# Merging the two score blocks of a sliding window into one place per key

## The chip, the cores and the metric

The kernel runs on one core of a Trainium2 chip. Its time is the device time of one execution in microseconds (us), taken as the median of several runs. The engines are TensorE (PE in the profile; PEld is its weight load, which overlaps), VectorE (DVE), ScalarE (ACT), GpSimd (POOL) and SyncE (SP, which issues the DMAs). PE, DVE, ACT and POOL each work through a queue of their own in order, and they wait for one another by semaphores.

## The reference

One inference step of a two-layer hybrid decoder for a prompt of 2048 tokens and for 8 single-token samples. Each layer normalises x, multiplies by W_in (1024 x 4880), runs three mixers on slices of the result (mLSTM, Mamba-2 SSD, sliding-window attention), gates them, and multiplies by W_out (1536 x 1024) with a residual. The change is in the attention over the prompt, of which this is the core (8 query heads, 2 key/value heads of 64, window 128):

```python
def _swa_prompt(q, k, v, sinks):
    ...
    kk = jnp.concatenate([jnp.pad(k, pad)[:, :-1], k], axis=2)
    vv = jnp.concatenate([jnp.pad(v, pad)[:, :-1], v], axis=2)
    s = jnp.einsum('nbqhgd,nbkhd->nbhgqk', q, kk).astype(F32) * (Dh ** -0.5)
    ...
    mask = (delta >= 0) & (delta < WINDOW) & (kpos >= 0)
    s = jnp.where(mask[None, :, None, None], s, -jnp.inf)
    p = _sink_softmax(s, sinks.reshape(HK, G)[:, :, None, None])
    o = jnp.einsum('nbhgqk,nbkhd->nbqhgd', p.astype(vv.dtype), vv)
```

A tile of 128 queries looks at 256 keys, its own 128 and the 128 of the tile ahead of it. Query i sees its own keys 0 to i and the neighbour's keys i+1 to 127. So of each pair of keys (own c, neighbour c) a query uses one alone.

## The kernel before, in words

The prompt is worked off in blocks of 512 tokens: four blocks in each of two layers, numbered n = 0 to 7. For a block PE multiplies the normalised x by column groups of W_in (`g0`, `qk`, `v`, `o`, `z`, `x0`, `x1`, `cq`, `cz`, `bz`), in chunks of 128 rows, and the mixed result by W_out (`out`). Each product of float32 values is made of three matmuls on split values (high x high, low x high, high x low), 12 matmuls of 512 columns to a chunk (L511 and L513, in `multiply`). In the first block of each layer the weights are loaded raw and split by ACT and POOL (L488, L491); later blocks load the parts back.

Between these matmuls a planner (`pump`) puts steps of the mixers: `mix_a` (mLSTM), `mix_b` (SSD), `mix_c` (attention). Each is a generator, and a step is issued when its stream's rate allows it and when a model of the engines (`Clock`, with the costs of `COST`) says that its inputs are there. At certain chunks the remaining steps of a stream are forced out (`drain`): stream c is drained before `out` of its own block begins; for the last block, where `out` follows with nothing else to do, before the eighth chunk of `out`. So the order of every engine's queue hangs on the planner's model, and a change in a step's instructions moves rows elsewhere too.

Attention is `mix_c`. For each of a block's four tiles, `pre_c` makes rotated and normalised q and k, transposes them and splits them; the rotation of q is on POOL (L1022 to L1025). `main_c` then does the following for each half a (4 heads that share a key head). `scores`: 8 matmuls of 128x256, and one DVE instruction for each head that adds a mask, writes the 128x256 scores to memory and leaves their maximum. `exps`: one ACT exponential for each head, with the sum. `norm`: one ACT scaling for each head. `turn(a, x)`, for the two key tiles x: four transposes on PE (L1171) into one PSUM bank, then the high part by ACT (L1173) and the low part by DVE (L1174). `values(a, x)`: two matmuls of 512 columns (L1180) for each x, four in all, into one accumulator. `out`: ACT, then DVE twice (L1187 to L1189). `parts` splits the tile's values into high and low, in `vs`. The very first tile of a layer has no neighbour (`nk` is 1). The scores' key slots alternate: `sl = c % 2` is the slot of the tile's own keys. `F[2:4]` and `F[4:6]` are single buffers for the transposed parts.

Of the kernel before, what the change touches and what calls it, by code (L numbers as in the profile page):

```python
# [11 lines left out]
F32 = mybir.dt.float32  # L12
# [17 lines left out]
NEG = -1e30  # L30
# [30 lines left out]
def host_consts():  # L61
    p = np.arange(128)
    ident = np.eye(128)
    triu = (p[:, None] <= p[None, :]).astype(np.float64)
    sel = np.zeros((128, 128))
    sel[127, :] = 1.0
    prev = np.where(p[None, :] > p[:, None], 0.0, NEG)
    cur = np.where(p[None, :] <= p[:, None], 0.0, NEG)
    lim = np.where(p[:, None] <= p[None, :], -NEG, 0.0)
    own = ((p[:, None] // 6 == np.arange(12)[None, :]) | (p[:, None] >= 72)).astype(np.float64)  # L70

    border = (np.arange(1, NT + 1) * 128 // (NT + 1))[None, :]
    coarse = np.concatenate([np.where(p[:, None] >= border, NEG, 0.0), p[:, None] < border], axis=1)
    cst = np.concatenate([ident, triu, sel, prev, cur, lim, own, coarse], axis=1).astype(np.float32)
# [92 lines left out]
class Build:  # L167
    def __init__(self, tc, ctx, I, O):
# [18 lines left out]
        self.mask = cp.tile([128, 384], F32, name="mask")  # L187
# [21 lines left out]
        self.vs = cp.tile([128, 2, 2, 128], F32R, name="vs")  # L209
        self.x1 = self.dr.tile([DM, SEQ], F32, name="x1")  # L210
# [8 lines left out]
    def consts(self):  # L219
# [5 lines left out]
        nc.sync.dma_start(self.mask[:, 0:256], c[:, 384:640])  # L225
        nc.sync.dma_start(self.mask[:, 256:384], c[:, 384:512])
# [887 lines left out]
    def main_c(self, S, c):  # L1114
# [3 lines left out]
        kz, vs = self.kz, self.vs  # L1118
# [4 lines left out]
        W = 128 * nk  # L1123
        mk = self.mask[:, 128:256] if first else self.mask[:, 0:256] if sl else self.mask[:, 128:384]
        Pu = [[u[:, 0:512].rearrange("p (j c) -> p j c", c=256) for u in us] for us in (U[8:10], [S['CQ'][c], U[10]])]
# [3 lines left out]
        def P(a, j):  # L1129
            return Pu[a][j // 2][:, j % 2, 0:W]  # L1130
# [4 lines left out]
        def scores(a):  # L1135
            mxr, nm, es, den = st[a]
            for j2 in range(2):
                pS = self.mx()
                for j in (2 * j2, 2 * j2 + 1):
                    o = pS[:, (j % 2) * 256:(j % 2) * 256 + W]  # L1140
# [3 lines left out]
                for j in (2 * j2, 2 * j2 + 1):  # L1144
                    nc.vector.tensor_tensor_reduce(P(a, j), pS[:, (j % 2) * 256:(j % 2) * 256 + W], mk, 1.0, NEG,
                                                   ALU.add, ALU.max, accum_out=mxr[:, j:j + 1])
# [21 lines left out]
        def turn(a, x):  # L1168
            pT = self.mx()
            for j in range(4):  # L1170
                nc.tensor.transpose(pT[:, j * 128:j * 128 + 128], P(a, j)[:, x * 128:x * 128 + 128], self.ident)  # L1171
            PTh, PTl = self.F[2 + 2 * x:4 + 2 * x]
            nc.scalar.activation(PTh, pT, AF.Copy)  # L1173
            TT(PTl, pT, PTh.bitcast(F32), op=ALU.subtract)  # L1174

        def values(a, x):
            if x == 0:
                pO[a] = self.mx()
            for i, p in enumerate(self.F[2 + 2 * x:4 + 2 * x]):
                nc.tensor.matmul(pO[a], vs[:, x, a, :], p, start=x == 0 and i == 0, stop=x == nk - 1 and i == 1)  # L1180
# [10 lines left out]
        def parts():  # L1191
# [3 lines left out]
            TT(parts[:, 1:3], v, parts[:, 0:4:3].bitcast(F32), op=ALU.subtract)  # L1195

        ops = [(0, 0, parts)]
        for a in range(2):
            o = 2 * a
            ops += [(o, 2, scores, a), (o + 1, 2, exps, a), (o + 2, 2, norm, a), (o + 3, 2, turn, a, 0)]  # L1200
            for x in range(nk):
                ops.append((o + 4 + x, 1, values, a, x))
                if x + 1 < nk:
                    ops.append((o + 4 + x, 2, turn, a, x + 1))
# [690 lines left out]
```

## Time and profile before

| | us |
|---|---|
| median of 3 runs (lowest to highest) | 3053.2 (3044.29 to 3054.06) |
| the profiled execution's own time | 3047.01 |
| its span, first to last instruction | 3044.9 |
| PE busy | 2944.7 |
| DVE busy | 1873.7 |
| ACT busy | 1248.7 |
| POOL busy | 720.6 |

The mean clock granted to TensorE is 0.989 of its 2.4 GHz. PE is busy for 97% of the span, in all but the first of forty slices. Matmuls are pipelined and their recorded ends overlap with the next one's start; what one costs the queue is the distance from start to start, which the chain of waits shows as it walks from one to the next.

### The profile page before, as it was taken

What the parts mean: (1) busy time and instruction counts of PE and PEld (TensorE: products, weight loads), DVE (VectorE), ACT (ScalarE), POOL (GpSimd) and SP (SyncE); (2) the same over time, 40 slices, a digit from 0 to 9 for tenths busy, and PEclk for the clock granted to TensorE, in tenths of its full rate; (3) what the DMA queues carried; (4) which work ended last, traced back from release to release, by engine and by line L of the source; (5) the groups of instructions that cost most, each with busy time, mean ns of one, the idle gap of its engine ahead of it and who ended that gap; (6) DMA issues with size and microseconds to landing.
All of it is one profiled execution on the core that took longest, in us unless ns stands there. A gap on an engine that the chain in (4) does not pass through costs nothing.

```text
span 3044.9 us, 42758 instructions
## 1 busy us (share of the span) xinstructions
PE 2944.7 (97%) x14722; PEld 2414.3 (79%) x14722; DVE 1873.7 (62%) x4630; ACT 1248.7 (41%) x3080; POOL 720.6 (24%) x808
## 2 busy tenths in 40 slices
PE   6999999999999999999999999999999999999998
PEld 5787878878778788887878778788888788888877
DVE  4249656676476764467644676576755677544774
ACT  4343554325532254324454334552354224532354
POOL 3336104341030310005330561141400222000300
PEclk9999999999999999999999999999999999999999
DMA  7865547855476454564565755587444854445533
GB/s 206 278 207 200 183 143 259 269 170 163 155 227 203 151 158 154 166 197 139 175 229 171 245 191 175 184 274 244 146 153 156 271 177 149 152 156 168 176 108 125
DMA packets 263837, 567.31 MB, mean 186 GB/s; under 512 B 67020, under 2 KB 100204, under 8 KB 263572
## 3 DMA queue, kind: packets, MB, share of 16 engines
q1 hardware_dynamic: 263620, 564.58, 57.5%
q8 instruction: 116, 1.90, 0.2%
q14 instruction: 101, 0.83, 0.1%
HBM read 434.72 MB, written 132.06 MB: 186 GB/s over the span
## 4 chain that ended last, share of the span: by engine, by line
PE 72%; DVE 10%; DMA 7%; issue 4%; POOL 3%; ACT 2%; SPq 1%; POOLq 0%; DVEq 0%; ACTq 0%
PE pj L511 30%; PE pj L513 27%; DMA wr<-in_w_in 2%; PE mx L1180 2%; PE mx L1143 2%; PE mx L1171 1%; PE mx L974 1%; POOL hl L491 1%; PE mx L1221 1%; PE mx L840 1%; PE mx L847 1%; PE mx L534 1%; PE mx L533 1%; DVE quad L649 1%; PE mx L983 1%
## 5 line engine op out<-in xcount | busy, mean ns | idle before, releaser
L513 PE MATMUL pj<-hl,xTh 128*128 128x512 f32 (+1 forms) x3072 | 959.5, 386 | 18.0 <-DVE quad L554 9.7
L511 PE MATMUL pj<-xTh,hl 128*128 128x512 f32 x2240 | 725.0, 401 | 3.3 <-ACT xTh L1228 3.1
L513 PEld LDWEIGHTS pj<-hl,xTh 128*128 128x128 f32 x3072 | 568.1, 191 | 129.5 <-DVE quad L554 11.6
L513 PE MATMUL pj<-hl,xTl 128*128 128x512 f32 (+1 forms) x1536 | 586.4, 384 | 0.0
L511 PE MATMUL pj<-parts,hl 128*128 128x512 f32 x2016 | 517.4, 404 | 10.8 <-ACT parts L1228 3.7
L511 PEld LDWEIGHTS pj<-xTh,hl 128*128 128x128 f32 x2240 | 420.9, 189 | 98.2 <-ACT xTh L1228 4.1
L511 PEld LDWEIGHTS pj<-parts,hl 128*128 128x128 f32 x2016 | 368.8, 189 | 91.0 <-DVE parts L1235 4.4
L511 PE MATMUL pj<-xTl,hl 128*128 128x512 f32 x1120 | 437.6, 400 | 0.0
L491 POOL TENSOR_TENSOR hl<-wr,hl 128x512 fp32r<-128x512 f32 (+1 forms) x208 | 283.5, 1368 | 435.0 <-ACT hl L488 376.7
L513 PEld LDWEIGHTS pj<-hl,xTl 128*128 128x128 f32 x1536 | 293.2, 191 | 52.6
L511 PEld LDWEIGHTS pj<-xTl,hl 128*128 128x128 f32 x1120 | 212.1, 190 | 44.7
L1235 DVE SCALAR_TENSOR_TENSOR parts<-quad,lp_ynw,parts 128x512 fp32r<-128x512 f32 x168 | 143.2, 855 | 164.2 <-ACT quad L1232 74.0
L488 ACT ACTIVATE hl<-wr 128x512 fp32r<-128x512 f32 (+1 forms) x208 | 126.4, 614 | 232.5 <-DMA wr<-in_w_in 75.8
L1158 ACT ACTIVATE unit<-unit,c_m,c_sc 128x256 f32<-128x256 f32 (+1 forms) x192 | 111.8, 583 | 86.5 <-DVE c_m L1149 86.4
L1228 ACT ACTIVATE parts<-quad,lp_ynw 128x512 fp32r<-128x512 f32 x112 | 80.5, 720 | 155.3 <-PE pj L511 146.4
L1174 DVE TENSOR_TENSOR parts<-mx,parts 128x512 fp32r<-128x512 f32 x124 | 84.5, 686 | 96.7 <-ACT parts L1173 94.6
L1022 POOL TENSOR_TENSOR unit<-quad,rpqn 128x256 f32<-128x256 f32 x32 | 24.1, 753 | 500.5 <-PE mx L941 225.7
L649 DVE SCALAR_TENSOR_TENSOR quad<-quad,lp_cw,quad 128x512 f32<-128x512 f32 x192 | 140.1, 774 | 0.3
L1173 ACT ACTIVATE parts<-mx 128x512 fp32r<-128x512 f32 x124 | 73.0, 594 | 107.5 <-PE mx L1171 105.1
L1180 PE MATMUL mx<-parts,vs 128*128 128x512 f32 x248 | 103.9, 434 | 7.7 <-ACT parts L1173 4.6
L393 POOL TENSOR_TENSOR quad<-quad 128x512 f32<-128x512 f32 x24 | 33.9, 1414 | 287.6 <-ACT quad L391 286.9
L977 POOL TENSOR_TENSOR hst<-hst,X 128x512 f32<-128x512 f32 x32 | 34.0, 1063 | 240.3 <-PE mx L955 234.5
(404 smaller groups left out, 4565.2 us busy)
## 6 DMA issues: line engine op xcount, KB each, us to landing
hl<-kept SPq DMA_DIRECT2D x576, 512.0 KB
kept<-hl SPq DMA_DIRECT2D x192, 512.0 KB
wr<-in_w_in SPq DMA_DIRECT2D x144, 256.0 KB
hl<-kept SPq DMA_DIRECT2D x48, 272.0 KB
wr<-in_w_out SPq DMA_DIRECT2D x32, 256.0 KB
quad<-in_xT SPq DMA_DIRECT2D x32, 256.0 KB
x<-quad SPq DMA_DIRECT2D x32, 256.0 KB
quad<-x SPq DMA_DIRECT2D x16, 512.0 KB
```

Of the source, the lines that this page charges most:

```text
L488: nc.scalar.activation(h, raw, AF.Copy)
L491: nc.gpsimd.tensor_tensor(lw, raw, h.bitcast(F32), op=ALU.subtract)
L511: nc.tensor.matmul(ps[t], w[:, tt], a, start=st and first, stop=en and last)
L513: nc.tensor.matmul(ps[t][:, :N], a[:, tt], w[:, :N], start=st and first, stop=en and last)
L649: nc.vector.scalar_tensor_tensor(acc, u[:, j:j + 512], cw[:, j, c:c + 1], acc, op0=ALU.mult, op1=ALU.add)
L1143: nc.tensor.matmul(o, q, kz[:, a, s, 0:nk, :].rearrange("p n c -> p (n c)"), start=s == 0, stop=s == 1)
L1158: nc.scalar.activation(P(a, j), P(a, j), AF.Exp, bias=nm[:, j:j + 1], scale=head(sc, a, j), accum_out=den[:, j:j + 1])
L1173: nc.scalar.activation(PTh, pT, AF.Copy)
L1174: TT(PTl, pT, PTh.bitcast(F32), op=ALU.subtract)
L1180: nc.tensor.matmul(pO[a], vs[:, x, a, :], p, start=x == 0 and i == 0, stop=x == nk - 1 and i == 1)
L1228: nc.scalar.activation(yh.rearrange("p (t c) -> p t c", c=128), pt, AF.Copy, scale=L['ynw'][:, k:k + 1])
L1235: nc.vector.scalar_tensor_tensor(yl.rearrange("p (t c) -> p t c", c=128), blk, L['ynw'][:, k:k + 1], yh.bitcast(F32).rearrange("p (t c) -> ...
```

## The change

For every tile with a neighbour, the two scores of a pair of keys are merged into one place before the maximum. ACT copies the own block's scores of two heads out of PSUM, and DVE writes the neighbour's over them wherever the key comes later than the query (`copy_predicated` with `later`). One `tensor_reduce` then takes the four maxima of a half. From there P is 128x128 for each head and not 128x256: exponentials and scalings are half as wide, and there is one `turn` for each half and not two. The values are made right by linearity. With one merged P, the two first matmuls go against the neighbour's values for all keys; then P is masked to the own keys (`own`, two POOL multiplications by `triu`) and two more matmuls go against the difference of own and neighbour's values, `vd`, which `parts` computes and splits (one ACT and three DVE instructions more). The tiles without a neighbour add the mask and multiply once.

```diff
         def scores(a):
...
-                for j in (2 * j2, 2 * j2 + 1):
-                    nc.vector.tensor_tensor_reduce(P(a, j), pS[:, (j % 2) * 256:(j % 2) * 256 + W], mk, 1.0, NEG,
-                                                   ALU.add, ALU.max, accum_out=mxr[:, j:j + 1])
+                pS = pS.rearrange("p (j n c) -> p j n c", n=2, c=128)
+                P2 = Pu[a][:, 2 * j2:2 * j2 + 2]
+                if first:
+                    TT(P2, pS[:, :, 0], self.cur.unsqueeze(1).to_broadcast([128, 2, 128]), op=ALU.add)
+                else:
+                    nc.scalar.activation(P2, pS[:, :, sl], AF.Copy)
+                    nc.vector.copy_predicated(P2, self.later.bitcast(I32).unsqueeze(1).to_broadcast([128, 2, 128]),
+                                              pS[:, :, 1 - sl])
+            nc.vector.tensor_reduce(mxr, Pu[a], AX.X, ALU.max)
...
-        def turn(a, x):
+        def turn(a):
             pT = self.mx()
             for j in range(4):
-                nc.tensor.transpose(pT[:, j * 128:j * 128 + 128], P(a, j)[:, x * 128:x * 128 + 128], self.ident)
-            PTh, PTl = self.F[2 + 2 * x:4 + 2 * x]
+                nc.tensor.transpose(pT[:, j * 128:j * 128 + 128], P(a, j), self.ident)
+            PTh, PTl = self.F[2:4]
...
+        def own(a):
+            for p, o in zip(self.F[2:4], self.F[4:6]):
+                p, o = [x.bitcast(F32).rearrange("p (j c) -> p j c", c=128) for x in (p, o)]
+                nc.gpsimd.tensor_tensor(o.bitcast(F32R), p, self.triu.unsqueeze(1).to_broadcast([128, 4, 128]), op=ALU.mult)
+
         def values(a, x):
             if x == 0:
                 pO[a] = self.mx()
+            v = vd[:, a] if x else vs[:, sl if first else 1 - sl, a]
             for i, p in enumerate(self.F[2 + 2 * x:4 + 2 * x]):
-                nc.tensor.matmul(pO[a], vs[:, x, a, :], p, start=x == 0 and i == 0, stop=x == nk - 1 and i == 1)
+                nc.tensor.matmul(pO[a], v, p, start=x == 0 and i == 0, stop=x == nk - 1 and i == 1)
...
         def parts():
...
+            if not first:
+                old = vs[:, 1 - sl].rearrange("p a (s d) -> p (a s) d", d=64).bitcast(F32)
+                d = U[10][:, 0:128].rearrange("p (a d) -> p a d", d=64)
+                TT(d, v, old[:, 0:4:3], op=ALU.subtract)
+                TT(d, d, old[:, 1:3], op=ALU.subtract)
+                parts = vd.rearrange("p a (s d) -> p (a s) d", d=64)
+                nc.scalar.activation(parts[:, 0:4:3], d, AF.Copy)
+                TT(parts[:, 1:3], d, parts[:, 0:4:3].bitcast(F32), op=ALU.subtract)
...
-            ops += [(o, 2, scores, a), (o + 1, 2, exps, a), (o + 2, 2, norm, a), (o + 3, 2, turn, a, 0)]
+            ops += [(o, 2, scores, a), (o + 1, 2, exps, a), (o + 2, 2, norm, a), (o + 3, 2, turn, a)]
             for x in range(nk):
                 ops.append((o + 4 + x, 1, values, a, x))
-                if x + 1 < nk:
-                    ops.append((o + 4 + x, 2, turn, a, x + 1))
+            if nk > 1:
+                ops.append((o + 3, 3, own, a))
```

What this does to PE's queue, at three places. The first is a tile in the second block of layer 0. L1171 is a transpose and L1180 a values matmul of before; in the change they are L1177 and L1194, and `vd` marks the two against the difference. Before:

```order
L1180 MATMUL mx_7176<-parts_94,vs 128x512
L1171 MATMUL mx_7179<-ident,unit_90 128x128 x2
L1180 MATMUL mx_7176<-parts_95,vs 128x512
L1171 MATMUL mx_7179<-ident,unit_91 128x128 x2
L721 MATMUL mx_7217<-MB_7078,sel 128x64
L1171 MATMUL mx_7245<-ident,quad_104 128x128 x2
L1171 MATMUL mx_7245<-ident,unit_92 128x128 x2
L513 MATMUL pj_7143<-hl_7252,xTh_114 128x512
```

With the change:

```order
L1194 MATMUL mx_7353<-parts_95,vs 128x512
L1177 MATMUL mx_7372<-ident,unit_92 128x128 x3
L1194 MATMUL mx_7353<-parts_96,vs 128x512
L1177 MATMUL mx_7372<-ident,unit_92 128x128
L1194 MATMUL mx_7353<-parts_97,vd 128x512
L1099 MATMUL mx_7395<-ident,unit_90 128x128 x2
L1102 MATMUL mx_7398<-ident,quad_105 128x128 x3
L1194 MATMUL mx_7353<-parts_98,vd 128x512
```

Two sets of four transposes stood between the first half's values, the neighbour's second set and the other half's first; now one stands there. The transposes that feed these values come earlier, and 22 matmuls of 512 columns (L514, before L513) stand between them and the first row shown.

The second place is PE's queue where block n = 6 is drained, just before its `out`. Before, from the last matmul ahead of the drained steps:

```order
L513 MATMUL pj_24053<-hl_24133,xTh_114 128x512
L1180 MATMUL mx_24204<-parts_94,vs 128x512
L1171 MATMUL mx_24207<-ident,unit_90 128x128 x2
L1171 MATMUL mx_24207<-ident,unit_91 128x128 x2
L1171 MATMUL mx_24245<-ident,quad_102 128x128 x2
L1171 MATMUL mx_24245<-ident,unit_92 128x128 x2
L1180 MATMUL mx_24204<-parts_95,vs 128x512
L1180 MATMUL mx_24204<-parts_96,vs 128x512
L1180 MATMUL mx_24254<-parts_94,vs 128x512
L1180 MATMUL mx_24204<-parts_97,vs 128x512
```

With the change:

```order
L1177 MATMUL mx_24118<-ident,unit_91 128x128 x4
L1194 MATMUL mx_24132<-parts_95,vs 128x512
L1177 MATMUL mx_24146<-ident,unit_92 128x128
L1194 MATMUL mx_24132<-parts_96,vs 128x512
L1177 MATMUL mx_24146<-ident,unit_92 128x128
L1194 MATMUL mx_24132<-parts_97,vd 128x512
L1177 MATMUL mx_24146<-ident,unit_92 128x128 x2
L1194 MATMUL mx_24132<-parts_98,vd 128x512
L1194 MATMUL mx_24155<-parts_95,vs 128x512
L1243 MATMUL mx_24163<-ident,quad_102 128x128 x4
L1194 MATMUL mx_24155<-parts_96,vs 128x512
L1243 MATMUL mx_24194<-ident,quad_102 128x128 x4
```

Before, the first set of transposes was spread over the matmuls ahead of the drain; now both halves' sets stand in it, with their values right behind them. The second half's scores end 12 matmuls of 512 columns ahead of the first row shown. L1243 turns another mixer's output for `out`.

The third place is the end of the last tile of the program, with what was the last of its values. Before:

```order
L1180 MATMUL mx_27078<-parts_94,vs 128x512
L1180 MATMUL mx_27038<-parts_97,vs 128x512
L1171 MATMUL mx_27081<-ident,quad_98 128x128 x2
L1180 MATMUL mx_27078<-parts_95,vs 128x512
L1171 MATMUL mx_27081<-ident,unit_92 128x128 x2
L511 MATMUL pj_26985<-xTl_116,hl_26941 128x512
L511 MATMUL pj_26986<-xTl_116,hl_26941 128x512
L511 MATMUL pj_26987<-xTl_116,hl_26941 128x512
L1180 MATMUL mx_27078<-parts_96,vs 128x512
L1180 MATMUL mx_27078<-parts_97,vs 128x512
```

With the change:

```order
L512 MATMUL pj_26809<-xTl_117,hl_26783 128x512
L1177 MATMUL mx_26926<-ident,unit_91 128x128 x4
L1194 MATMUL mx_26940<-parts_95,vs 128x512
L1177 MATMUL mx_26954<-ident,unit_92 128x128 x4
L1194 MATMUL mx_26940<-parts_96,vs 128x512
L1194 MATMUL mx_26940<-parts_97,vd 128x512
L1194 MATMUL mx_26963<-parts_95,vs 128x512
L1194 MATMUL mx_26940<-parts_98,vd 128x512
L1194 MATMUL mx_26963<-parts_96,vs 128x512
L1194 MATMUL mx_26963<-parts_97,vd 128x512
L1194 MATMUL mx_26963<-parts_98,vd 128x512
```

Before, only the second half's second key tile was left at the end, behind three other matmuls. Now both halves' transposes and all eight values matmuls stand together, with no other matmul among them; what follows in both cases is the part of `out` that needs this tile. The change has 240 transposes fewer on PE (of 496 on L1171), 120 instructions more on POOL, and as many values matmuls as before.

## Rows read from the trace of the kernel before

**Rows 1.** The page: span; busy time, share and instructions of each engine.

```profile
span 3044.9 us, 42758 instructions
...
PE 2944.7 (97%) x14722; PEld 2414.3 (79%) x14722; DVE 1873.7 (62%) x4630; ACT 1248.7 (41%) x3080; POOL 720.6 (24%) x808
```

**Rows 2.** PE's waits: who waited for whom, us in all, times, longest.

```profile
PE mx L443 <- DVE quad L1824: 16.5, 1, 16.5
PE mx L974 <- DVE unit L969: 12.3, 6, 4.6
```

**Rows 3.** Groups of PE by line: names, shapes, count, busy, mean ns, idle before.

```profile
L1171 PE MATMUL mx<-ident,unit 128*128 128x128 f32 x372 | 70.9, 277 | 6.0 <-ACT unit L1166 5.4 <-DVE unit L966 0.6
...
L1171 PE MATMUL mx<-ident,quad 128*128 128x128 f32 x124 | 24.8, 274 | 0.0
```

**Rows 4.** The chain that ended last: start, us, what, how many.

```profile
2966.59 5.58 PE pj L511 x24
2972.17 0.23 PE mx L1180
2972.40 0.44 PE mx L1171 x4
```

**Rows 5.** Groups of DVE by line and shape: count, busy, mean ns, idle before.

```profile
L1174 DVE TENSOR_TENSOR parts<-mx,parts 128x512 fp32r<-128x512 f32 x124 | 84.5, 686 | 96.7 <-ACT parts L1173 94.6 <-PE mx L1180 1.5
L1145 DVE CUSTOM_DVE_ANT_0 unit<-mx,mask 128x256 f32<-128x256 f32 x180 | 67.8, 420 | 24.7 <-PE mx L1143 24.3
...
L1038 DVE TENSOR_REDUCE qn<-unit 128x8 f32<-128x512 f32 x32 | 21.3, 679 | 48.7 <-ACT unit L1034 48.6
...
L1145 DVE DVE_READ_ACCUMULATOR2_ANT c_m<- 128x1 f32 x256 | 21.1, 82 | 0.0
```

**Rows 6.** ACT by line: ns min/median/max, start, forms.

```profile
L1158 ACT ACTIVATE unit<-unit,c_m,c_sc x192: 477/587/605, 325.9 to 2998.2; 128x256 f32<-128x256 f32 x180, 128x128 f32<-128x128 f32 x12
...
L1166 ACT ACTIVATE unit<-unit,c_m x192: 385/494/516, 329.0 to 3000.7; 128x256 f32<-128x256 f32 x180, 128x128 f32<-128x128 f32 x12
```

**Rows 7.** ACT, groups by line and shape, as in rows 5.

```profile
L1173 ACT ACTIVATE parts<-mx 128x512 fp32r<-128x512 f32 x124 | 73.0, 594 | 107.5 <-PE mx L1171 105.1 <-DVE mst L727 1.2
...
L1104 ACT ACTIVATE kz<-mx 128x256 fp32r<-128x256 f32 x32 | 12.1, 379 | 23.2 <-PE mx L1098 23.0
```

**Rows 8.** POOL, groups by line and shape, as in rows 5.

```profile
L491 POOL TENSOR_TENSOR hl<-wr,hl 128x512 fp32r<-128x512 f32 x192 | 270.6, 1414 | 394.6 <-ACT hl L488 336.4 <-DMA hl<-kept 27.2 <-DMA wr<-in_w_in 12.0
L1024 POOL TENSOR_TENSOR quad<-quad,rpqn 128x512 f32<-128x512 f32 x32 | 42.9, 1342 | 4.4 <-ACT unit L1034 3.5
...
L979 POOL TENSOR_TENSOR unit<-unit,X 128x512 f32<-128x512 f32 x32 | 34.1, 1064 | 156.5 <-PE mx L974 151.4 <-ACT parts L1109 5.1
...
L1022 POOL TENSOR_TENSOR unit<-quad,rpqn 128x256 f32<-128x256 f32 x32 | 24.1, 753 | 500.5 <-PE mx L941 225.7 <-DVE qn L1038 208.1 <-DVE ltB L781 66.7
```

**Rows 9.** DVE line L1149: ns min/median/max.

```profile
L1149 DVE TENSOR_TENSOR c_m<-c_m,lp_nsink x64: 125/161/1199, 325.7 to 2995.4; 128x4 f32<-128x4 f32 x64
```

**Rows 10.** Instructions in order of time, POOL and DVE near 1829 us.

```profile
1828.96 1.28 POOL L491 TENSOR_TENSOR hl<-wr,hl 128x512 fp32r<-128x512 f32 x1
...
1829.06 1.20 DVE L1149 TENSOR_TENSOR c_m<-c_m,lp_nsink 128x4 f32<-128x4 f32 x1
```

**Rows 11.** PE in order of time, at the drain of block 6.

```profile
2661.42 0.50 PE L1180 MATMUL mx<-parts,vs 128*128 128x512 f32 x1 [0.71 <-ACT parts L1173]
```

**Rows 12.** PE's waits from 2880 to 2955 us, as in rows 2.

```profile
PE mx L1180 <- ACT parts L1173: 1.6, 2, 0.9
```

**Rows 13.** Stretches: length, busy PE, PEld, DVE, ACT, POOL; granted clock; DMA.

```profile
2931.00:2937.00 6.00, 5.36 (x24) 5.20 (x24) 3.13 (x15) 3.55 (x12) 0.00 (x0) 0.50 0.00 0
3008.00:3015.00 7.00, 3.89 (x17) 2.45 (x16) 3.80 (x6) 3.00 (x5) 0.00 (x0) 1.00 0.38 135
```

**Rows 14.** The chain that ended last, behind the last tile's values.

```profile
3011.71 0.60 ACT unit L1187
...
3014.55 12.97 PE pj L511 x48
```

More of the change, by code (lines that the diff above doesn't have):

```diff
@@ L66, in host_consts @@
     sel[127, :] = 1.0
-    prev = np.where(p[None, :] > p[:, None], 0.0, NEG)
+    later = (p[None, :] > p[:, None]).astype(np.float64)
     cur = np.where(p[None, :] <= p[:, None], 0.0, NEG)
@@ L73, in host_consts @@
     coarse = np.concatenate([np.where(p[:, None] >= border, NEG, 0.0), p[:, None] < border], axis=1)
-    cst = np.concatenate([ident, triu, sel, prev, cur, lim, own, coarse], axis=1).astype(np.float32)
+    cst = np.concatenate([ident, triu, sel, later, cur, lim, own, coarse], axis=1).astype(np.float32)
     inv = (10000.0 ** (-np.arange(32) / 32.0)).astype(np.float32)
@@ L186, in __init__ @@
         self.sel = cp.tile([128, 128], F32, name="sel")
-        self.mask = cp.tile([128, 384], F32, name="mask")
+        self.later, self.cur = [cp.tile([128, 128], F32, name=n) for n in ("later", "cur")]
         self.identb = cp.tile([128, 128], BF16, name="identb")
@@ L209, in __init__ @@
         self.vs = cp.tile([128, 2, 2, 128], F32R, name="vs")
+        self.vd = cp.tile([128, 2, 128], F32R, name="vd")
         self.x1 = self.dr.tile([DM, SEQ], F32, name="x1")
@@ L224, in consts @@
         nc.sync.dma_start(self.sel, c[:, 256:384])
-        nc.sync.dma_start(self.mask[:, 0:256], c[:, 384:640])
-        nc.sync.dma_start(self.mask[:, 256:384], c[:, 384:512])
+        nc.sync.dma_start(self.later, c[:, 384:512])
+        nc.sync.dma_start(self.cur, c[:, 512:640])
         t = self.U[7]
@@ L1117, in main_c @@
         QT = self.F[0:2]
-        kz, vs = self.kz, self.vs
+        kz, vs, vd = self.kz, self.vs, self.vd
         first = b == 0 and c == 0
@@ L1122, in main_c @@
         nk = 1 if first else 2
-        W = 128 * nk
-        mk = self.mask[:, 128:256] if first else self.mask[:, 0:256] if sl else self.mask[:, 128:384]
-        Pu = [[u[:, 0:512].rearrange("p (j c) -> p j c", c=256) for u in us] for us in (U[8:10], [S['CQ'][c], U[10]])]
+        Pu = [u[:, 0:512].rearrange("p (j c) -> p j c", c=128) for u in U[8:10]]
         st = [[self.s([128, 4], f"c_m{i}") for i in range(4)] for _ in range(2)]
@@ L1129, in P @@
         def P(a, j):
-            return Pu[a][j // 2][:, j % 2, 0:W]
+            return Pu[a][:, j]
         def head(x, a, j):
@@ L1139, in scores @@
                 for j in (2 * j2, 2 * j2 + 1):
-                    o = pS[:, (j % 2) * 256:(j % 2) * 256 + W]
+                    o = pS[:, (j % 2) * 256:(j % 2) * 256 + 128 * nk]
                     q = QT[a][:, j * 128:j * 128 + 128]
```

## The prediction

> **What bounds the kernel now.** I read the page first: PE is busy for 2944.7 of 3044.9 us, and no other engine passes 62% [rows 1]. Then PE's waits: of the 100 us in which it is idle, 16.5 lie at the start, before the first transposes can run, and the next longest entry is 12.3 [rows 2]. Nothing waits for long, so time is won by giving PE fewer columns to stream, and lost where PE's queue stands still. Then the groups by line, for what the edited instructions take [rows 3, 5 to 8]; the chain, for what a matmul costs PE's queue from start to start [rows 4]; and the places where the attention runs with little beside it: the drain of block 6, the start of the last block, and the last tile [rows 11 to 14].
>
> **PE: what goes.** 30 of the 32 tiles have a neighbour; each has two halves with two sets of four transposes, and the other two tiles have one set for each half: 124 sets, 496 transposes [rows 3]. With the change it is 64. A set of four costs the queue 0.44 us, as one 512-column values matmul costs 0.23 and 24 main matmuls 5.58 (0.2325 each) [rows 4]. So 60 x 0.44 = 26.4 us of queue leave PE. The upper end is the busy time of the groups, (70.9 + 24.8) / 124 = 0.77 us a set, 46 us for 60 [rows 3]; but recorded ends of pipelined matmuls overlap, so I take 0.44. Score and values matmuls stay as many and as wide. The lower end is nothing, if waits fill all that is freed.
>
> **DVE.** 240 maximum instructions of 128x256 go (0.420 each, and 0.082 for the accumulator read), and 60 subtractions of `turn` (0.686): 120.5 + 41.2 = 161.7 us [rows 5]. 120 predicated copies come. The trace has none of them; the nearest row is the maximum itself, which also streams 256 PSUM scores and a mask: 0.420. The lower end is nothing beyond the 0.082 of a one-column read, the upper twice 0.420 if the copy first has to read what it overwrites [rows 5]. At 0.420 they take 50.4. 64 reductions of 128x512 at 0.679 take 43.5 [rows 5], and 90 small operations of `parts` at most 0.42 each, 37.8. DVE ends about 30 us lighter, 20 heavier at the upper end: of 62% it is a percent either way.
>
> **ACT.** Exponentials and scalings halve in width. 240 of each go from 0.587 to 0.477 and from 0.494 to 0.385 (the minima of these rows are the 128x128 form): 26.4 + 26.2 us [rows 6]. 60 copies of `turn` go at 0.594, 35.6; 120 copies out of PSUM come at 0.379, 45.5, and 30 small ones at no more, 11.4 [rows 7]. ACT ends 31 us lighter. All this lies beside PE's main matmuls, as the sums of before do; I count nothing for it. Where the cover is gone, in a drain, the change costs or saves a single instruction's length, and there it is counted below.
>
> **POOL.** 120 multiplications of 128x512 come. By the nearest row, which also broadcasts one input, each takes 1.342 us; the ends are 1.064 and 1.414 [rows 8]. That is 161 us (128 to 170) on an engine busy for 721 [rows 1].
>
> **What hides POOL's work.** The one new wait: the last two values matmuls of a half wait for POOL, and behind them in PE's queue stand main matmuls that would be ready. From the last transpose it takes 0.594 (ACT) + 1.342 = 1.9 us to the first masked part and 3.3 to the second [rows 7, 8]. In the second block's tile the queue holds 22 + 2 matmuls and one set of transposes between the last transpose and the first of these two values: 24 x 0.2325 + 0.44 = 6.0 us [rows 4]. Cover is 4.1 us of other POOL work, three operations of 1.34. At most tiles the wait costs nothing. The cover is gone in the drains.
>
> **Drain of block 6.** Both halves now stand there together. The second half's scores end 12 matmuls, a set and a value ahead of its transposes: 2.79 + 0.44 + 0.23 = 3.5 us. What must happen in between: two copies 0.76, the last predicated copy 0.42, the reduction 0.68, three small DVE operations of 0.16 [rows 9], four exponentials 1.91, two small operations 0.32, four scalings 1.54: 6.1 [rows 5 to 7]. PE waits 2.6 us here; the wait for ACT's 0.594 lies inside it. Then the single buffer is refilled: POOL's first operation, from 0.59 to 1.94 us behind the first set, is over by then, and the second half's high part costs another 0.5 us or so. So 3.1, where before PE waited 0.7 [rows 11]: +2.4 us.
>
> **Last tile.** Four POOL operations stand in one line behind the first transposes: 0.594 + 4 x 1.342 = 6.0 us to the last values matmul. PE has a set of transposes and seven values in that time, 0.44 + 7 x 0.23 = 2.05, and stands for 3.9. The chain behind it stays: from the end of the last values at 3011.7 to the next matmul at 3014.55 are 2.9 us [rows 14]. Before, PE stood for 7.00 - 3.89 = 3.1 us around it, that is 0.2 beside this chain [rows 13]. So +3.7 us.
>
> **Start of the last block.** Values waited 1.6 us for ACT's copies [rows 12]. Half of these copies are gone, and transposes of `out` now fill in: a first wait of 0.6 is left, -1.0 us.
>
> **Sum.** -26.4 + 2.4 + 3.7 - 1.0 = -21.3, against the profiled execution's 3047.0: 3025.7 us. That execution lies 6.2 us below the median of the runs shown, 3053.2, and 2.7 above the lowest; I put the forecast between the two bases, at 3028 us.
>
> **The port between DVE and POOL.** At 1829.06 us a DVE multiplication of four columns, whose median is 0.161 us, took 1.20 while POOL was in one that began at 1828.96 and ran 1.28 [rows 9, 10]. Both its inputs are in SBUF. So a POOL operation can hold DVE for its whole length. "SBUF — State Buffer" in the Trainium skill, section "Who interferes with whom", says that a DVE instruction with two SBUF inputs contends with a GpSimd instruction that reads SBUF, and that whoever comes first has the ports for the whole instruction. By that rule, which the row agrees with, the 120 multiplications speak against the change.
>
> **Rivals.**
> 1. *POOL holds DVE.* 120 x 1.342 = 161 us more in which DVE's instructions with two SBUF inputs stand; if half of it holds one, DVE gets 80 us and gives back its 30, 1924 of 3025, 64%. DVE is not the bound, but PE waits for it, 12.3 us on L974 alone [rows 2]. POOL's busy time grows by 161/721, 22%. If all idle time of PE behind its start, 100.2 - 16.5 = 83.7 us, hung on DVE and grew by as much, it would be 18 us; at half of that 9: 3037. For it: the row above. Against it: `copy_predicated` and the subtraction of `turn` read PSUM.
> 2. *The planner's new order makes new waits.* The rows of all engines move. What a bad place costs shows at 2931 to 2937 us: PE, which had stood there before, was granted 0.50 of its clock, the lower of its two levels, 1.2 GHz, and streamed at half speed, 3 us lost in 6 [rows 13]. Together with waits like that of L974 (4.6 at longest, [rows 2]) such a place is worth about 8 us. Two of them more than before bring 3028 + 16 = 3044, no change against 3053 once the base is 3047. Against it: the freed room on PE is the same everywhere, and old places can vanish as well, up to the 12.3 us of L974, 3016.
> 3. *Values wait for POOL everywhere: slower.* POOL's queue has the rotation of the next tile's q, two operations of 0.753 and two of 1.342, 4.2 us [rows 8]. If it stands between a half's transposes and its masking, it passes the cover of 4.1 us; with the six table operations before it, or a second loaded queue in the blocks that split weights (1.414 each), the wait grows by 1.3 us for every operation over three. It decides from one such operation at 60 halves: 60 x 1.34 = 80 us would give 3108; at the 24 halves ahead of a next tile's rotation, 24 x 1.34 = 32 us and 3060, slower. Against it: in POOL's queue as ordered, what stands directly ahead of a masking is a single multiplication of another mixer, a split of weights, a memset or the other half's masking, not a rotation.
> 4. *The freed time comes back as idle:* the other mixers' DVE and ACT work or the loading of weights sets the pace, and what PE no longer streams it waits: all 26.4 us of it give 3052 and, with the two gains and losses of the drains, no change. For it: the stretches where DVE is what PE waits for. Against it: the longest such wait after the start is 4.6 us [rows 2], and DVE and ACT lose work too.
>
> **Chances and range.** The forecast (3015 to 3038) has 0.62, rival 1 0.12, rival 2 0.13 (half of it ends as no change), rival 3 0.08, rival 4 0.05. The range from 3012 to 3047 holds the sum with both bases, the good end of rival 2 and its bad end; above it lie rivals 3 and 4. A difference under 0.3%, 9 us, is what the runs of this kernel can't tell from none. Faster: 0.62 + 0.12 + half of rival 2 = 0.80, less 0.03 for the scatter of the base: 0.77. No change: half of rival 2, rival 4 and half of this scatter, 0.13. Slower: rival 3 and the other half, 0.10.
>
> **What would show it.** In the profile after, the transposes' line should have 256 instructions, PE's busy time be lower by about 26 us or more, and POOL's higher by 128 to 170. The two `vd` matmuls of a middle tile should start with no wait for POOL; at the drain of block 6 and at the last tile they should wait, about 3 and 4 us. DVE's busy time would be about 30 us lower; if it is not lower, the predicated copy or the port was mispriced. The forecast is wrong if PE's idle time grows by more than 15 us, or if a `vd` matmul waits for POOL in most tiles.

## The result, and the profile after

The kernel after takes 3016.8 us (median of 4 runs, 3012.6 to 3019.8) against 3048.7 for the kernel before beside it (4 runs, 3042.7 to 3054.1): a ratio of 0.9890, 95% interval 0.9867 to 0.9913, or 32 us less. The two profiled spans differ by 34.1 us, 3044.9 [rows 1] and 3010.8. The page of the kernel after, its part 1 (busy time, share, instructions):

```profile
span 3010.8 us, 42267 instructions
...
PE 2915.7 (97%) x14482; PEld 2386.1 (79%) x14482; DVE 1900.8 (63%) x4340; ACT 1219.5 (41%) x3170; POOL 882.7 (29%) x928
```

Against [rows 1], PE is busy 29.0 us less with 240 matmuls fewer, and its idle time falls from 100.2 to 95.1. ACT loses 29.2 us, POOL gains 162.1, and DVE, which was to lose 30, gains 27.1.

The groups of the kernel after by line, engine and shape (busy time, mean ns, idle time ahead and what ended it). Lines have shifted: the transposes of L1171 are now L1177, the values of L1180 are L1194, and L1186 is POOL's masking.

```profile
L1186 POOL TENSOR_TENSOR parts<-parts,triu 128x512 fp32r<-128x512 f32 x120 | 159.3, 1343 | 426.7 <-ACT parts L1179 405.6 <-DVE parts L1180 13.7 <-DVE rq_t L327 2.0
...
L1203 DVE TENSOR_TENSOR quad<-quad,unit 64x512 f32<-64x512 f32 x64 | 56.7, 886 | 1.7
L970 DVE SCALAR_TENSOR_TENSOR unit<-unit,unit 128x512 f32<-128x512 f32 x64 | 56.2, 919 | 0.7
L1150 DVE COPY_PREDICATED unit<-later,mx 128x256 f32<-128x256 int32 x120 | 51.1, 444 | 19.5 <-ACT unit L1149 18.5
...
L1152 DVE TENSOR_REDUCE c_m<-unit 128x4 f32<-128x512 f32 x64 | 43.7, 682 | 0.9
...
L1164 ACT ACTIVATE unit<-unit,c_m,c_sc 128x128 f32<-128x128 f32 x256 | 124.2, 487 | 78.0 <-DVE c_m L1155 77.5
...
L1172 ACT ACTIVATE unit<-unit,c_m 128x128 f32<-128x128 f32 x256 | 81.9, 394 | 17.1 <-DVE c_m L1170 16.6 <-ACT parts L1179 0.3
...
L1194 PE MATMUL mx<-parts,vd 128*128 128x512 f32 x120 | 50.8, 439 | 0.9 <-POOL parts L1186 0.7
...
L1177 PE MATMUL mx<-ident,unit 128*128 128x128 f32 x256 | 46.9, 280 | 5.5 <-ACT unit L1172 5.5
```

The 256 transposes answer to the two groups of [rows 3]. The predicated copy takes 0.444 us, the reduction 0.682, a half exponential 0.487 and a half scaling 0.394 (0.420, 0.679, 0.477 and 0.385 were assumed). The values matmuls that read `vd` waited for POOL for less than a microsecond in all 120. What became longer are instructions that the change doesn't touch, such as L1203 and L970. In the kernel before the same two groups, then L1189 and L969, read:

```profile
L969 DVE SCALAR_TENSOR_TENSOR unit<-unit,unit 128x512 f32<-128x512 f32 x64 | 51.0, 837 | 0.8
...
L1189 DVE TENSOR_TENSOR quad<-quad,unit 64x512 f32<-64x512 f32 x64 | 45.8, 716 | 1.4
```

PE's longest waits after, as in [rows 2] (us in all, times, longest):

```profile
PE mx L444 <- DVE quad L1846: 15.9, 1, 15.9
PE mx L975 <- DVE unit L970: 12.4, 6, 5.5
PE pj L514 <- DVE quad L555: 6.1, 6, 2.5
...
PE mx L1177 <- ACT unit L1172: 5.5, 1, 5.5
PE mx L1194 <- ACT parts L1179: 4.7, 3, 2.6
```

The list has the same shape as before: the start, the wait of L975 for DVE, and some entries of 4 to 6 us. No new line tops it.

The last tile in the order of time (start, duration, engine, line, idle time ahead and its releaser). It answers to [rows 13, 14]:

```profile
2971.37 0.50 PE L1194 MATMUL mx<-parts,vs 128*128 128x512 f32 x1 [1.33 <-ACT parts L1179]
2971.40 4.98 POOL L1186 TENSOR_TENSOR parts<-parts,triu 128x512 fp32r<-128x512 f32 x4 [18.25 <-ACT parts L1179]
...
2976.44 0.49 PE L1194 MATMUL mx<-parts,vd 128*128 128x512 f32 x1 [0.72 <-POOL parts L1186]
...
2979.82 2.50 PE L512 MATMUL pj<-xTh,hl 128*128 128x512 f32 x5 [2.89 <-ACT xTh L1250]
```

POOL's four operations stand in one line from 2971.40 for 4.98 us, and the last values matmul starts when the fourth is over. PE stands 1.33 us for ACT's copy, 0.22 for DVE, 0.72 for POOL, and then 2.89 for the chain behind the tile: 5.2, where it stood 3.1 before. Its values matmuls are recorded with 0.49 to 0.50 us each. That is no lower clock: the granted clock was 1.00 here, as it was around the last tile before [rows 13], where a matmul with nothing ready behind it is recorded with as much. Start to start in a full queue one costs 0.23 [rows 4]. After (columns as in [rows 13]), and then before:

```profile
2971.00:2977.00 6.00, 4.29 (x12) 1.93 (x12) 3.13 (x4) 1.55 (x4) 4.98 (x4) 1.00 0.15 62
```

```profile
3011.17 0.50 PE L1180 MATMUL mx<-parts,vs 128*128 128x512 f32 x1 [0.23 <-DVE parts L1174]
```

So the busy time of a row of lone matmuls overstates what they are worth, and idle time alone understates what such a place costs.

### The profile page after: what moved, and what is told of

Read it like the earlier page. It is cut to its first block, busy times and chain, and to the rows that moved or that the text cites. A ratio compares the mean times of both kernels' runs of the same rounds, so it can differ in the third digit from the quotient of the medians.

```text
span 3010.8 us, 42267 instructions
## 1 busy us (share of the span) xinstructions
PE 2915.7 (97%) x14482; PEld 2386.1 (79%) x14482; DVE 1900.8 (63%) x4340; ACT 1219.5 (41%) x3170; POOL 882.7 (29%) x928
## 4 chain that ended last, share of the span: by engine, by line
PE 74%; DVE 11%; DMA 7%; POOL 2%; issue 2%; ACT 2%; SPq 1%; POOLq 0%; DVEq 0%; ACTq 0%
PE pj L512 30%; PE pj L514 28%; PE mx L1194 2%; DMA wr<-in_w_in 2%; PE mx L1143 2%; PE mx L975 1%; POOL hl L492 1%; PE mx L535 1%; PE mx L534 1%; DMA kept<-hl 1%; PE mx L1243 1%; PE mx L1177 1%; DMA unit<-bcd 1%; PE mx L841 1%; PE mx L862 1%
## 5 line engine op out<-in xcount | busy, mean ns | idle before, releaser
L514 PE MATMUL pj<-hl,xTh 128*128 128x512 f32 (+1 forms) x3072 | 946.2, 383 | 11.1 <-DVE quad L555 6.1
L514 PEld LDWEIGHTS pj<-hl,xTh 128*128 128x128 f32 x3072 | 566.3, 190 | 122.2 <-DVE quad L555 7.7
L514 PE MATMUL pj<-hl,xTl 128*128 128x512 f32 (+1 forms) x1536 | 582.2, 382 | 0.0
L514 PEld LDWEIGHTS pj<-hl,xTl 128*128 128x128 f32 x1536 | 291.4, 190 | 52.3
L1186 POOL TENSOR_TENSOR parts<-parts,triu 128x512 fp32r<-128x512 f32 x120 | 159.3, 1343 | 426.7 <-ACT parts L1179 405.6
L1164 ACT ACTIVATE unit<-unit,c_m,c_sc 128x128 f32<-128x128 f32 x256 | 124.2, 487 | 78.0 <-DVE c_m L1155 77.5
L1180 DVE TENSOR_TENSOR parts<-mx,parts 128x512 fp32r<-128x512 f32 x64 | 43.9, 686 | 76.7 <-ACT parts L1179 74.5
L534 PE MATMUL mx<-hl,samS 128*66 128x512 f32 (+1 forms) x208 | 84.9, 409 | 4.5 <-ACT hl L489 4.5
L1172 ACT ACTIVATE unit<-unit,c_m 128x128 f32<-128x128 f32 x256 | 81.9, 394 | 17.1 <-DVE c_m L1170 16.6
```

Source lines behind the costliest of these rows:

```text
L514: nc.tensor.matmul(ps[t][:, :N], a[:, tt], w[:, :N], start=st and first, stop=en and last)
L534: nc.tensor.matmul(pd[:66, :N], self.samS[:, k, :], hi[:, :N], start=st, stop=False)
L1164: nc.scalar.activation(P(a, j), P(a, j), AF.Exp, bias=nm[:, j:j + 1], scale=head(sc, a, j), accum_out=den[:, j:j + 1])
L1172: nc.scalar.activation(P(a, j), P(a, j), AF.Copy, scale=den[:, j:j + 1])
L1186: nc.gpsimd.tensor_tensor(o.bitcast(F32R), p, self.triu.unsqueeze(1).to_broadcast([128, 4, 128]), op=ALU.mult)
```

## The experiments

All runs are timed against the kernel before on their own chip (medians 3049.5 to 3050.5 there). Differences below are to the kernel after: ratio minus 0.9890, times 3050.

The order of the queues is made in two places. The planner writes the steps, and then the framework's own scheduler, which has a model of durations, sorts the rows of each engine once more. To change an instruction and nothing else, both must be held: instructions that are added are hidden from the planner, and ordering edges between neighbours of one engine (they add no wait) hold all five queues as in the kernel after:

```
+        if at in self.unseen:
+            continue
...
+            for i in [mine[at]] + new.get((e, at), []):
...
+                if prev is not None:
+                    tc.add_manual_dep(i, prev.name, info(), reason="queue")
+                prev = i
```

In the three runs that are called free below, the second part is missing. Their expectations speak of held queues, but only the planner was held: 471 rows of PE's queue moved in the first and 645 in the last. The same edits were then run held.

**The transposes given back**, free, and then held:

```
             for j in range(4):
                 nc.tensor.transpose(pT[:, j * 128:j * 128 + 128], P(a, j), self.ident)
+            if nk > 1:
+                for j in range(4):
+                    nc.tensor.transpose(pT[:, j * 128:j * 128 + 128], P(a, j), self.ident)
```

> The changed kernel with every engine's queue held in its own order, and the set of four transposes written twice (60 more sets, unseen by the planner): the transposes of the kernel before, in the order of the kernel after. Theory: the gain is PE's columns, 0.44 us for a set, and what goes beyond is the new order: +26 us on 3017, 3043, ratio to before 0.998. Rival A (a set costs the queue more than its columns, the whole 32 us of the gain are these 60 sets, 0.53 each): +32, 3049, ratio 1.000. Rival B (the gain is order alone, and transposes fill time in which PE waits anyway): below +8, ratio 0.992 or less.

> As the first try, now with every engine's queue really held in the changed kernel's order (in the first calls the framework's own scheduler had still moved 471 rows of PE's queue): 60 sets of four transposes more, nothing else. Theory: PE's columns, 0.44 us a set, +26 on the kernel after; with the ratio of the kernel after, 0.989, that is 0.9975. The first try gave +20, with the order free; then order is worth 6 us here. Rival A (a set costs 0.53): 1.000. Rival B (the transposes fill waits): 0.992 or less.

Free: 3036.8 us, 0.9963 (0.9950 to 0.9976), +22 us by the ratio. Held: 3039.2, 0.9964 (0.9951 to 0.9977), +23; the intervals of the two ratios together leave 15 to 31. The page of the held run (this execution is 7 us longer than their median):

```profile
span 3044.7 us, 42750 instructions
...
PE 2946.2 (97%) x14722; PEld 2415.4 (79%) x14722; DVE 1901.8 (62%) x4340; ACT 1216.6 (40%) x3170; POOL 882.8 (29%) x928
```

The other three engines are within 3 us of the kernel after, so this is PE alone. From start to start in PE's queue, its 496 transposes fill 55.2 us in the trace and the 256 of the kernel after 28.8: 26.4 us for 60 sets, 0.44 each. (In the trace of the kernel before, in its own order, the 496 fill 50.7, 21.9 more than after.) So rival B falls (the transposes don't fill waits), and the theory's 26 lies inside the interval; rival A's 32 lies just outside it. Neither run gives back the whole gain.

**POOL's work taken away, and moved to DVE.** The first masks 2 of each 128 columns and leaves out the other 126.

```
-                nc.gpsimd.tensor_tensor(o.bitcast(F32R), p, self.triu...to_broadcast([128, 4, 128]), op=ALU.mult)
+                nc.gpsimd.tensor_tensor(o[:, :, 0:2].bitcast(F32R), p[:, :, 0:2], self.triu[:, 0:2]..., op=ALU.mult)
```

> The changed kernel, queues held, POOL's 120 multiplications cut to 2 of each 128 columns, so that the masked parts are wrong and their time on POOL is gone (a memset of the buffers at the start of each layer is added). Theory: DVE falls by the 57 us of POOL's hold to about 1844, and PE gains only the waits of the drains, 1 to 4 us: ratio 0.988. Rival (POOL holds DVE and PE waits for that): 0.986 or less.

Measured: 3014.9, 0.9887 (0.9868 to 0.9907), 1 us below the kernel after. Its page, and two of DVE's groups:

```profile
PE 2914.2 (97%) x14482; PEld 2384.6 (79%) x14482; DVE 1857.9 (62%) x4342; ACT 1215.1 (40%) x3170; POOL 753.3 (25%) x928
```

```profile
L1343 DVE TENSOR_TENSOR quad<-quad,unit 64x512 f32<-64x512 f32 x64 | 48.3, 755 | 1.7
...
L1108 DVE SCALAR_TENSOR_TENSOR unit<-unit,unit 128x512 f32<-128x512 f32 x64 | 50.7, 832 | 0.7
```

DVE falls by 42.9 us, and the two groups (L1203 and L970 of the kernel after) go back from 886 to 755 ns and from 919 to 832. So POOL did hold DVE. PE's gain from its letting go is 1 us by the ratio, and the two intervals leave 9 either way; PE is idle for 98.0 us in this trace, against 95.1 in the kernel after, so its waits in sum didn't shrink. The theory holds, and the rival by which PE waits for this finds no support.

```
-                nc.gpsimd.tensor_tensor(o.bitcast(F32R), p, self.triu...to_broadcast([128, 4, 128]), op=ALU.mult)
+                nc.vector.tensor_tensor(o.bitcast(F32R), p, self.triu...to_broadcast([128, 4, 128]), op=ALU.mult)
```

> The changed kernel, queues held, with the two multiplications of a half on DVE, directly behind its subtraction, and not on POOL. They read two inputs in SBUF, as the subtraction for xTl does (0.736 us): 120 x 0.736 = 88 us more for DVE, 57 less if POOL's hold on it goes, so DVE at about 1932, POOL at 723. Theory: no change beside other work, 2 to 4 us gained in the drains, 3013 to 3016, ratio 0.988. Rival (DVE is what PE waits for): 1.5 us more in DVE's queue for each half delays what stands behind it, +8 us or more, ratio 0.992 or above.

> The changed kernel, queues held, the two multiplications of a half on DVE directly behind its subtraction. With the order free: 3 us slower than the kernel after, DVE at 1934. Theory: what DVE takes on (88 us) and what POOL no longer holds (57) are both beside PE's work; the drains gain 2 to 3: ratio 0.988, as in the kernel with POOL's time taken away. Rival (1.5 us more in DVE's queue for each half makes PE wait): 0.991 or above.

Free: 3020.1, 0.9904 (0.9891 to 0.9917). Held: 3020.2, 0.9904 (0.9886 to 0.9922), +4 us, which these intervals can't tell from none. Page and group of the held run:

```profile
PE 2917.3 (97%) x14482; PEld 2386.1 (79%) x14482; DVE 1930.7 (64%) x4460; ACT 1214.9 (40%) x3170; POOL 727.7 (24%) x808
```

```profile
L1325 DVE TENSOR_TENSOR parts<-parts,triu 128x512 fp32r<-128x512 f32 x120 | 82.1, 725 | 0.0
```

1930.7 - 82.1 = 1848.6 us is what DVE has to do when POOL doesn't mask: 52 us under the kernel after (43 with the narrow masks, which still take some of POOL's time), and 25 under the kernel before, close to the 30 that the prediction had. The gain of 2 to 3 us in the drains that the theory wanted didn't come, nor the rival's loss with any certainty.

**POOL's work doubled**, each multiplication issued twice:

```
                 nc.gpsimd.tensor_tensor(o.bitcast(F32R), p, self.triu...to_broadcast([128, 4, 128]), op=ALU.mult)
+                nc.gpsimd.tensor_tensor(o.bitcast(F32R), p, self.triu...to_broadcast([128, 4, 128]), op=ALU.mult)
```

> The changed kernel, queues held, with each of POOL's multiplications issued twice: POOL at 1043 us. A half's second part is then over 0.594 + 4 x 1.342 = 6.0 us behind the transposes, as much as the cover of 6.0. Theory: the cover is used up, values wait a few tenths in many tiles and 1.3 to 5.4 us more in the two drains: +8 to +16 us, 3025 to 3033, ratio 0.992 to 0.995; DVE's busy time grows by another 57 us. Rival (POOL's work has free room, and PE never waits for it beside the drains): +3 to +7. Rival (POOL holds DVE and PE waits for that): over +16.

> The changed kernel, queues held, each of POOL's multiplications issued twice. With the order free this was 26 us slower than the kernel after, with DVE 48 us busier and 645 rows of PE's queue moved. Theory now: the cover is used up and DVE is held longer; of the 26 the larger part is new order, so held +8 to +14, ratio 0.992 to 0.9935. Rival (it is POOL's time itself, through late values or through DVE): +20 or more, ratio 0.9955 or above.

Free: 3043.1, 0.9978 (0.9968 to 0.9988), +27. Held: 3064.4, 1.0042 (1.0024 to 1.0060), +46. My theory falls, and the rival with 20 us or more holds. The theory missed both in its 8 to 14 us and in its claim that the new order was the larger part of the loss: with the order held the loss is larger, and the scheduler, left free, had hidden 20 us of it. The held run's page and PE's waits:

```profile
span 3061.9 us, 42382 instructions
...
PE 2933.3 (96%) x14482; PEld 2392.7 (78%) x14482; DVE 1944.5 (64%) x4340; ACT 1215.4 (40%) x3170; POOL 1047.1 (34%) x1048
```

```profile
PE mx L1335 <- POOL parts L1326: 19.5, 13, 3.0
...
PE mx L1113 <- DVE unit L1108: 13.9, 7, 5.6
```

The span grows by 51.1 us: 33.5 of idle time and 17.6 of busy time. The new entry is the first row, 13 waits of `vd` values for POOL, 19.5 us. The longest entry for DVE (L1113 is L975 of the kernel after) hardly moves, though DVE is busy for another 44 us. But summed over the list, PE's waits for DVE grow from 57.0 us (31 waits) to 67.4 (42), spread over entries that gain 2.6 at most. So the late values are the larger part of the new idle time; whether the 10 us of waits for DVE come from POOL's hold on it or only follow from the other delays was not separated. The busy time grows with the same matmuls, because PE runs longer at its lower level. Mean granted clock of the kernel after and of this one:

```profile
core 0: 3010.8 us, clock 0.987
```

```profile
core 0: 3061.9 us, clock 0.982
```

As an estimate from these rows, 0.013 of 3010.8 is 39 us lost to the clock, 0.018 of 3061.9 is 55: 16 us more, nearly the 17.6. Which stretches were lower, and after which waits, was not followed one by one.

**Other orders, same instructions.** One constant of the planner's model is changed, in the kernel before and in the kernel after:

```
-    HOP = 250.0
+    HOP = 240.0
```

> The kernel before with one constant of the planner's model, the 250 ns between two engines, set to 240: the same instructions in another order (506 rows of PE's queue moved, against 1293 by the change itself). Theory: the order alone is worth several us either way, 3 to 15 from 3049, so that the 8 to 11 us by which the gain exceeds the transposes (22 held) lie within it. Rival (the order is worth under 3 us, and the rest of the gain is ACT's and DVE's shorter work): 3046 to 3053, ratio 0.999 to 1.001.

> The kernel before with that constant at 260 (208 rows of PE's queue moved). Theory: 3 to 10 us either way from 3049. Rival: 3046 to 3053.

> The kernel after with that constant at 240 (890 rows of PE's queue moved). Theory: 3 to 15 us either way from 3017, more likely above it than below, since this order of the kernel after is 8 to 11 better than its transposes explain: 3014 to 3032, ratio 0.988 to 0.994. Rival (order is worth under 3 us): 0.988 to 0.990.

> The kernel after with that constant at 260 (259 rows of PE's queue moved). Theory: 3 to 10 us either way, 3010 to 3027, ratio 0.987 to 0.9925. Rival: 0.988 to 0.990.

Before: 1.0040 (1.0027 to 1.0053) and 1.0018 (1.0010 to 1.0027), 12 and 5 us slower than with 250. After: 3039.8, 0.9967 (0.9955 to 0.9979), and 3029.9, 0.9936 (0.9923 to 0.9948), 23 and 14 us slower. The page of the kernel after with 240 (its profiled execution is the longest of six, 8 us above their median, and that of the kernel after is 4 below its own):

```profile
span 3045.8 us, 42276 instructions
...
PE 2929.7 (96%) x14482; PEld 2392.4 (79%) x14482; DVE 1905.2 (63%) x4340; ACT 1216.4 (40%) x3170; POOL 882.5 (29%) x928
```

Of the 35 us between the two spans, 21.0 are PE's idle time (116.1 for 95.1), spread over many entries of which none gains more than 3.5, and 14.0 are busy time with the same matmuls. The rival falls, in the kernel before with 260 only just. The theory holds for the kernel before; for the kernel after its direction does, but both sizes were missed: 3 to 15 and 3 to 10 us were expected. An order is worth 5 to 23 us here, where the change is worth 32. Over the three orders the means are 3056 for the kernel before and 3029 for the kernel after, 27 us apart.

**A mended drain.** At the last tile of blocks 6 and 7 the low part's mask goes to DVE, all queues held:

```
+                e = nc.vector if S['n'] > 5 and c == 3 and k == 1 else nc.gpsimd
+                e.tensor_tensor(o.bitcast(F32R), p, self.triu...to_broadcast([128, 4, 128]), op=ALU.mult)
```

> The kernel after, queues held in its order, with one thing moved: at the last tile of blocks 6 and 7, where the steps stand in a drain, the low part's multiplication is on DVE (0.68 us in the run with all of them there) and only the high part's on POOL. In the last tile four POOL operations in one line (4.98 us) become two beside DVE's two; the last values matmul should start some 1.1 us sooner after the first transposes, and block 6 gain up to 1. Theory: 3013 to 3017, ratio 0.987 to 0.989, that is 1 to 2 us below the kernel after and hardly to be told from it; it also times the order of the kernel after once more. Rival (the drain's wait is set by ACT's copies and DVE's own subtraction): no gain, 0.989, and the last values matmul starts as late as before.

Measured: 3015.9, 0.9887 (0.9867 to 0.9907), which can't be told from the kernel after. In its last tile:

```profile
2973.84 0.51 PE L1337 MATMUL mx<-parts,vs 128*128 128x512 f32 x1 [1.32 <-ACT parts L1317]
...
2977.75 0.19 PEld L1337 LDWEIGHTS mx<-parts,vd 128*128 128x128 f32 x1 [0.36 <-DVE parts L1326]
```

From the first values matmul to the weights of the last it takes 3.9 us, against 5.1 for the same step above: 1.15 us sooner, as reckoned. At block 6 the wait for ACT's copy stayed at 2.6 us, as the rival had it. This kernel beats the kernel before and equals the kernel after. As a second timing of the same order it also bears out the 0.989.

## Why the prediction was right, and where it was wrong

**PE, what goes: right.** 60 sets at 0.44 us were put at 26.4. Start to start in the traces they fill 26.4 in the held run. By time they gave back 23, within 15 to 31.

**What hides POOL's work: right, and narrow.** The cover was put at 6.0 us for a need of 1.9 and 3.3. One masking for each part costs 1 us in all, give or take 9 (POOL's work taken away); two for each part cost 46, with 13 waits. Rival 3 was a real mechanism, kept away by the room that was left. One sign that the prediction gave didn't show: the `vd` matmuls were to wait for POOL about 3 and 4 us in the two drains, and they waited 0.7 in the last tile and not at all at block 6.

**DVE: wrong.** It was to be 30 us lighter and is 27 heavier. The new operations cost what was assumed, so the step that failed is the sum that left POOL's hold out: 43 to 52 us of it, by the runs with narrow masks and with the masks on DVE. The prediction had the mechanism as rival 1, at 80 us if half of POOL's time held one. A row in the kernel after, DVE and POOL at one place, shows how it looks:

```profile
2183.41 0.67 DVE L1202 TENSOR_TENSOR unit<-unit,mx 64x512 f32<-64x512 f32 x1
...
2185.55 0.67 DVE L1203 TENSOR_TENSOR quad<-quad,unit 64x512 f32<-64x512 f32 x1
2186.14 1.26 DVE L698 COPY li<-kvg 128x16 f32<-128x16 f32 x1
```

```profile
2183.59 1.30 POOL L1186 TENSOR_TENSOR parts<-parts,triu 128x512 fp32r<-128x512 f32 x1 [4.81 <-ACT parts L1179]
2185.70 1.68 POOL L1186 TENSOR_TENSOR parts<-parts,triu 128x512 fp32r<-128x512 f32 x1 [0.81 <-DVE parts L1180]
```

At 2186.14 a copy of 16 columns takes 1.26 us and ends as POOL's multiplication does, at 2187.38; its line has a median of 0.174. At 2183.41 an addition that reads PSUM, L1202, takes its usual 0.67 beside another. So POOL's hold isn't kept to DVE instructions with two inputs, of which the prediction spoke. "SBUF — State Buffer" in the Trainium skill, section "Who interferes with whom", says so too: a copy can run in a mode that takes both of DVE's ports, and then contends. The row agrees with it; whether this copy ran in that mode no view shows. Rival 1's price for PE, 9 to 18 us, doesn't show: with the hold gone the kernel gained 1 us, give or take 9, and PE's idle time didn't fall.

**ACT: right**, 29 us lighter for 31. **POOL: right**, 1.343 us each for 1.342, 162 in all for 161.

**The drains: mis-sized, and at block 6 by another path.** By idle time they look cheap: PE stands 5.2 us around the last tile, 2.1 more than before, and 2.6 at the drain of block 6, 1.9 more. But lone matmuls hide part of the loss in busy time, and so does a lower clock. Timed from start to start, from the first transposes of the drained steps (before: from the last main matmuls ahead) to the next main matmul behind them, the two places read as follows, block 6 first. Columns as in [rows 13]. Before:

```profile
2660.31:2666.34 6.03, 5.11 (x29) 3.46 (x27) 4.53 (x9) 5.13 (x12) 0.00 (x0) 1.00 0.35 121
3009.51:3014.55 5.04, 1.93 (x8) 0.84 (x6) 3.35 (x6) 2.16 (x5) 0.00 (x0) 1.00 0.31 104
```

After:

```profile
2622.99:2632.85 9.86, 7.21 (x24) 4.73 (x23) 6.02 (x12) 7.49 (x23) 5.21 (x4) 0.66 0.17 55
2968.93:2979.82 10.89, 5.41 (x18) 2.40 (x17) 4.54 (x7) 4.96 (x13) 4.98 (x4) 0.90 0.17 64
```

At 0.11 us for a transpose and 0.23 for any other matmul, what starts in them would take 4.0 and 1.2 us before, and 3.4 and 2.7 after. So 2.0 and 3.9 us were lost before, and 6.5 and 8.2 after: +4.5 at block 6 and +4.3 at the last tile, where +2.4 and +3.7 were forecast.

At block 6 the wait of 2.6 us came out as worked out, but by luck. The prediction had the second half's transposes wait for its scalings. In the trace the first half's values wait for ACT's copy of their transposes, which stands in ACT's queue behind the second half's four exponentials; the scalings come after it:

```profile
2622.99 0.60 PE L1177 MATMUL mx<-ident,unit 128*128 128x128 f32 x4
...
2623.56 0.49 ACT L1164 ACTIVATE unit<-unit,c_m,c_sc 128x128 f32<-128x128 f32 x1
...
2625.57 0.59 ACT L1179 ACTIVATE parts<-mx 128x512 fp32r<-128x512 f32 x1
...
2626.22 0.79 PE L1194 MATMUL mx<-parts,vs 128*128 128x512 f32 x1 [2.63 <-ACT parts L1179]
...
2626.53 1.29 ACT L1172 ACTIVATE unit<-unit,c_m 128x128 f32<-128x128 f32 x4
```

POOL doesn't stand in the list of waits there. Behind this wait PE went on at the lower level of its clock: the mean granted clock of the stretch is 0.66, where it was 1.00 before. The prediction's sum has nothing for that.

**Start of the last block: wrong sign.** A wait of 5.5 us for the scaling stands there now (L1177 in the waits above), where 1.0 was to be gained. One stands there in all three orders of the kernel after (5.5, 4.3 and 4.5 us) and in none of the three of the kernel before, which waits there in L974 (3.9, 3.9 and 5.6), so it is not a matter of one order.

**The size, 3016.8 for 3028.** The sum gave -21.3, and 32 were measured. The transposes account for 22 to 26. The drains take back 9 and POOL about 1, so that 16 to 20 us were won elsewhere, which the sum didn't have. Two stretches hold most of them, each marked off by the same 100 main matmuls of PE in both traces. Before:

```profile
383.40:426.60 43.20, 37.63 (x187) 30.85 (x186) 26.99 (x111) 24.41 (x63) 3.12 (x5) 0.92 0.30 106
748.70:791.30 42.60, 37.79 (x181) 31.03 (x181) 24.48 (x97) 30.10 (x81) 3.86 (x5) 0.92 0.32 110
```

After:

```profile
380.40:413.30 32.90, 32.90 (x168) 27.16 (x167) 19.90 (x56) 13.53 (x37) 6.61 (x9) 1.00 0.44 135
734.60:766.70 32.10, 32.10 (x166) 26.66 (x165) 25.02 (x95) 15.85 (x46) 8.14 (x7) 1.00 0.46 149
```

They take 85.8 us before and 65.0 after. 36 transposes fewer are 4 of these 20.8 us; otherwise the stretches hold nearly the same matmuls (368 in all before, 334 after). PE was idle for 10.4 us in them before (5.4 of it a wait of L1171 for the scaling of L1166) and not at all after, and with the waits the lower clock went, 0.92 on average for 1.00. So the good end of rival 2, 3016, came on top of the forecast's mechanism: old places vanished, though not the one that it named, since the wait for DVE that was L974's 12.3 us is still 12.4. That the forecast's own sum stayed near is in part luck, because the drains cost more than it had and these places gave more.

Why they vanished is not shown. They are of the size that other orders of the same instructions cost (5 to 23), and in both kernels the order as given was the best of three. Another order of the kernel before (240) takes 73.5 us for the two stretches. But the three orders of the kernel after all take 65 to 66 and none of the kernel before does, and ACT, for which PE waited there, is busy for 54.5 us in them before and 29.4 after. So the change itself, by ACT's shorter chains or by less attention at these places, may have done it as well as the order; no run separates the two. Over the whole kernel TensorE's clock brought nothing, since its mean was 0.989 before and 0.987 after.

## What to carry to other kernels

Where one engine is busy for 97%, a change is worth what it takes out of that engine's queue, start to start, and work put on an idle engine is free until its result comes later than the queue's cover: measure that margin by doubling the work, since beyond it the loss came at once, as waits and as a lower clock. Idle time is a poor measure of a place where matmuls stand alone: time it from start to start. Where a scheduler orders the rows, a single build carries a draw of the order, 0.2 to 0.8% here beside a change of 1.1%; hold the queues, or look at a few orders, before the difference is put down to an edit. A sum of busy times of an engine that shares a port must carry what its neighbour holds.

## What the runs showed of the hardware that was not expected

A POOL multiplication of 128x512 held even a DVE copy of 16 columns with one input, 1.26 us for 0.17 (one row). A predicated copy of 128x256 from PSUM takes 0.444 us, hardly more than the 0.420 of a maximum with a mask. POOL's own multiplications, mostly 1.29 us, took up to 1.75 in the kernel after (1.68 in the row above).
